# Attention products with v, retention scores and k-v products placed in larger groups, weight splits of four blocks

## Chip, core and metric

One Trainium2 chip, one core. The time is the device time of one execution in microseconds. Before the change it was 1318.73 us, the median of 3 runs (1318.46 to 1319.16). The engines have short names: PE is TensorE (matrix products), DVE is VectorE, ACT is ScalarE, POOL is GpSimd, and SP is SyncE, which issues the transfers (DMA).

## What is computed

One inference step of a two-layer encoder over 512 prompt frames and 32 sample frames, 544 columns in all, model width 1024. Each layer runs three branches side by side, merges them through gates, and ends in a layer norm. Cut to what matters here:

```python
def layer(x, pe, pos, w_in, rel_table, ...):
    u = x @ w_in
    qa, ka, va, za, qb, kb, vb, zb, xr, zc, ga, gb, gc = split_cols(u)
    # A: softmax attention with a bias by distance
    scores = einsum(qa * d ** -0.5, ka) + rel_bias;  ya = softmax(scores) @ va
    ya = ya * silu(za)
    # B: retention in blocks, rotary q and k
    inner = einsum('bnihd,bnjhd->bnhij', qb, kb) * decay
    y_in  = einsum('bnhij,bnjhe->bnihe', inner, vb)
    kv    = einsum('bnjhd,bnjhe,hj->nbhde', kb, vb, zeta)   # then a scan gives s_prev
    y_x   = einsum('bnihd,nbhde,hi->bnihe', qb, s_prev, xi)
    yb = group_norm_heads(y_in + y_x) * silu(zb)
    # C: conv and a gated linear recurrence, yc = ... * silu(zc)
    merged = sigmoid(ga) * (ya @ w_branch[0]) + sigmoid(gb) * (yb @ w_branch[1]) + sigmoid(gc) * (yc @ w_branch[2])
    r = ALPHA * x + merged @ w_out
    r = r + sigmoid(r @ w_ple_gate) * (pe @ w_ple)
    return layer_norm(r, ln_gain, ln_bias), ...
```

There are 8 heads of width 64 in A and in B. All of it is in f32; the prompt and the sample share the weights.

## The kernel before, in words

**Main stream.** All large weights are cut into blocks of 128 x 128 and stored in the order in which they are used; eight blocks are a chunk of 512 KB. A weight block and an activation are each held as a sum of two reduced-precision parts, h and lo (names ending in h and l). `block` (line 244) multiplies h by xh, h by xl and lo by xh, each over the 544 columns in two spans of 288 and 256: six products, all recorded under line 253. A unit of work (`layer_units`) is one tile of 128 output rows, with 2, 4 or 8 blocks accumulated in PSUM, after which `evac` takes the result out.

**Weights.** `load` (line 189) brings a chunk into a buffer of the pool `wr` (the name raw, four buffers; the DMA is line 201). `split` (line 206) makes two blocks at a time: a cast on ScalarE gives h (line 208), a subtraction on VectorE gives lo (line 209). Both go to the pool `wp` (wh and wl), or, for the gate weights and those of the last products of a layer, to a slab (held). `stream` (line 216) runs the splits ahead of use, at least `LEAD` = 8 blocks, and calls `load` for the next chunk when the last part of one is split. `split_ahead` (line 235) loads and splits the first four chunks of layer 1 while the end of layer 0 runs; their DMA is line 238.

**Order.** It is written out by hand: the instructions of each engine run in the order in which the program emits them. Small jobs (Python generators) run beside the main stream. `tick` is called once per block; each job says with `yield n` that it goes on n blocks later, and `PACE` holds these numbers. So what a job emits at once stands as a small group between the products of two blocks.

**Attention.** `attn_job` (line 362) adds a step every 8 blocks (`PACE["step"]`), three steps for each of four head pairs, for query tiles (0, 1), (2) and (3). `attn_step` (line 380) emits the scores of both heads (line 393, name sc), then the softmax on VectorE and ScalarE, then for each head the transposes of the probabilities (line 409, name tp) with a copy back, and at the end the products with v (line 420, name pv, probabilities sx, v as vatok). From its scores to its products with v a step lasts 14 blocks, so two steps overlap. `sample_job` does the same for the 32 sample frames (scores L450, cached keys kvc).

**Retention.** `ret_job` forms k-v products per block of frames (line 583), the running states, then for each of four head pairs the scores (line 646, QB and KB), a mask on VectorE, the products with v (line 660, inner) and with the states (line 664), both into one PSUM tile.

In the profile's rows a product has the part of the array that it uses: 128\*128 is the whole array, 128\*64 one half of its columns, 64\*128 one half of its rows.

Of the kernel before, what the change touches and what calls it, by code (L numbers as in the profile page):

```python
# [55 lines left out]
def blocks_of(kind):  # L56
# [67 lines left out]
def encoder(ctx: ExitStack, tc, xT, pT, W, RB, KC, VC, PAR, CST, LGB, o_y, o_k, o_v, o_rp, o_rs, o_cv, o_lr):  # L124
# [5 lines left out]
    slab = pool("slab", 15)  # L130
    wr = pool("wr", 4)
    wp = pool("wp", LEAD // 2 + 3)
    tp_ = pool("tmp", 13)
    sm = pool("sm", 6)
# [70 lines left out]

    def split(n, h, lo):
        t = raw[n // 8][:, n % 8:n % 8 + 2]
        S.copy(h, t)  # L208
        V.tensor_tensor(lo, t, h.bitcast(F32), SUB)  # L209
        parts[n // 2] = (h, lo)  # L210

    def hold(n):
        held[n // 8] = sl("held", F32R, (128, 2, 8, 128))
        return [[held[n // 8][:, i, k:k + 2] for i in range(2)] for k in range(0, 8, 2)]

    def stream(lead=LEAD):
        while at["split"] < L * NB and at["split"] <= at["use"] + at["more"] + lead:
            n = at["split"]
            kind, f, k = BLOCKS[n % NB]
            if n // 2 not in parts:  # L220
                if kind == "wg" or kind == "pg" and f >= HELD[n // NB]:
                    if n % 8 == 0:
                        at["hold"] = hold(n)
                    h, lo = at["hold"][n % 8 // 2]
                else:
                    h = wp.tile([128, 2, 128], F32R, tag="wh", name="wh")
                    lo = wp.tile([128, 2, 128], F32R, tag="wl", name="wl")
                split(n, h, lo)
                if n % 8 == 6:
                    load()  # L230
            at["split"] += 2


    def split_ahead(l):
        for c in range((l + 1) * NCH, (l + 1) * NCH + (AT["xr"] + 16) // 8):
            t = wr.tile([128, 8, 128], F32, tag="raw", name="raw")
            raw[c] = t
            Q.dma_start(out=t, in_=W[c // NCH, c % NCH])
            views = hold(8 * c)
            yield 8  # L240
            for i, v in enumerate(views):
                split(8 * c + 2 * i, *v)
                yield 3

    def block(ps, xh, xl, first, last, hfs=(0, 1), n=None):
        if n is None:
            n = at["use"]
            at["use"] += 1
        h, lo = parts[n // 2]
        for i, (w, x) in enumerate(((h, xh), (h, xl), (lo, xh))):  # L250
            for hf in hfs:
                a, b = SPANS[hf]
                T.matmul(ps[:, MM0 + a:MM0 + b], lhsT=w[:, n % 2, :], rhs=x[:, a:b],  # L253
                         start=first and i == 0, stop=last and i == 2)
# [38 lines left out]
    for k in range(0, 8, 2):  # L293
        if k < 6:
            load()
        Q.dma_start(out=x0[k // 4][:, k % 4:k % 4 + 2], in_=xT[:, k:k + 2])
# [23 lines left out]
    def layer(l, env, nxt):  # L320
# [40 lines left out]
        def attn_job():  # L361
            while not all(k in env for k in ("vatok", "gates", ("K", 0))):
                yield 2
            env["ya"] = sl("ya")
            bias_loads(0)
            yield 4
            for p in range(4):
                while ("K", p) not in env:
                    yield 2
                for j in range(2):  # L370
                    G.memset(env["bias", p, j][0:64, 448:512], NEG)
                for qs in ((0, 1), (2,), (3,)):
                    if qs[0] == 2 and p < 3:
                        bias_loads(p + 1)
                    add(attn_step(p, qs))
                    yield PACE["step"]
            yield PACE["attn_end"]
            env["ya1"] = True

        def attn_step(p, qs):  # L380
            QTh, QTl, KTh, KTl = (env[k] for k in ("QTh", "QTl", "KTh", "KTl"))
            scs, xs, todo = [psum("sc") for _ in range(2)], [], []
            o = 0
# [22 lines left out]
            for j in range(2):  # L406
# [3 lines left out]
                copy("p%d" % j)(xs[j][:, :o], tp[:, :o])  # L410
                yield PACE["at3"]
            if qs[0] == 0:
                env["pv"] = psum("pv")
# [72 lines left out]
        def lru_tile(t):  # L486
# [12 lines left out]
            for g in range(2):  # L499
                w, lo = ([parts[(l * NB + AT["wg"] + g * 4 + t) // 2][i][:, t % 2] for i in range(2)])  # L500
                ps = psum("sc"), psum("pv")
# [61 lines left out]
        def ret_job():  # L563
# [13 lines left out]
            kvs = tmp("kvs", (128, 4, 64))  # L577
            for c in range(5):
                ps = psum("sc")
                for p in range(4):  # L580
                    for j in range(2):
                        hs = slice((2 * p + j) * 64, (2 * p + j) * 64 + 64)
                        T.matmul(ps[64 * j:64 * j + 64, p * 64:p * 64 + 64],  # L583
                                 lhsT=kt[:, c, hs] if c < 4 else kts[:, hs],
                                 rhs=vt[:, c, hs] if c < 4 else vts[:, hs], tile_position=(0, 64 * j))
                copy("kv")(kv[:, 4 * c:4 * c + 4] if c < 4 else kvs, ps[:, :256].rearrange("p (a b) -> p a b", a=4))
                yield PACE["kv"]
            mu = sm.tile([128, 64], F32, tag="mu", name="mu", bufs=1)
# [50 lines left out]
            yield 2  # L639
            for p in range(4):  # L640
                inn, scs = [], [psum("sc") for _ in range(2)]
                for c in range(4):
                    cc = slice(c * 128, c * 128 + 128)
                    for j in range(2):
                        r = slice(64 * j, 64 * j + 64)
                        T.matmul(scs[j][:, cc], lhsT=KB[r, p, cc], rhs=QB[r, p, cc])  # L646
                for sc in scs:
                    x = tmp("inner", (128, 512))
# [5 lines left out]
                pv = psum("pv")  # L654

                for c in range(4):
                    cc = slice(c * 128, c * 128 + 128)
                    for j in range(2):
                        h = 2 * p + j
                        T.matmul(pv[64 * j:64 * j + 64, cc], lhsT=vt[:, c, h * 64:h * 64 + 64], rhs=inn[j][:, cc],  # L660
                                 start=c == 0, stop=False)
                for c in range(1, 4):
                    cc = slice(c * 128, c * 128 + 128)
                    T.matmul(pv[:, cc], lhsT=std[:, (c - 1) * 4 + p], rhs=QB[:, p, cc], start=False, stop=c == 3)  # L664
                copy("yb")(QB[:, p, :NP], pv)
# [440 lines left out]
```

## Time and profile before

| | |
|---|---|
| time, median of 3 runs | 1318.73 us |
| the profiled execution | 1319.27 us |
| its span in the trace | 1317.2 us |
| granted TensorE clock, mean | 0.997 |
| DMA queue with the weights, share of 16 engines | 28.8% |
| HBM read and written over the span | 91 GB/s |

The span runs from the first to the last event of the trace; the execution's own time is 2.1 us longer. Busy time is a share of the whole span; which engine sets the end is read from what each one waits for. In a timeline row the columns are the start, the time from the first start to the last end, the engine, the line of the kernel, the operation, what it writes and reads, the shape, and how many instructions the row holds; in brackets stands the idle time before it and what ended it. The rows overlap on TensorE, since products are pipelined, so durations there are read from start to start.

### The profile page before, as it was taken

The page shows a single profiled execution, that of the slowest core. Times are in us where ns is not written, and L with a number is a line of the kernel's source. Part 1 is how long each engine was busy: PE and PEld are TensorE (multiplying, and loading weights), DVE is VectorE, ACT ScalarE, POOL GpSimd, SP SyncE. Part 2 cuts the span into 40 slices and gives each one's busy share as a digit, 9 for nine tenths or more (in the row PEclk, how much of TensorE's full clock was granted, in tenths as well). Part 3 has the DMA queues.
Part 4 walks back from the last instruction along what each step waited for, and adds up shares of the span by engine and source line. Part 5 has one row for each costly group of instructions (what it writes and reads, how often), then busy time and mean ns, then how long its engine had stood idle before and what let it go on. Part 6 is the DMA issues. An engine that isn't in the chain of part 4 may idle for free.

```text
span 1317.2 us, 26576 instructions
## 1 busy us (share of the span) xinstructions
PE 1299.4 (99%) x10744; PEld 1265.1 (96%) x10744; DVE 757.1 (57%) x1649; ACT 581.5 (44%) x1447; POOL 164.4 (12%) x158
## 2 busy tenths in 40 slices
PE   9999999999999999999999999999999999999996
PEld 9998889999999999999989998999999999999996
DVE  5666563583764453466584765636638544444567
ACT  6765544432742233334277655444326423333341
POOL 0210030320101101100032101213201011010000
PEclk9999999999999999999999999999999999999998
DMA  7233422231122222224212345132212222222221
GB/s 296 65 131 92 162 67 94 86 105 50 65 97 97 82 80 97 94 99 145 65 47 68 115 98 177 61 99 81 89 65 75 87 96 81 97 81 97 81 97 68
DMA packets 43465, 125.96 MB, mean 96 GB/s; under 512 B 9360, under 2 KB 11664, under 8 KB 42576
## 3 DMA queue, kind: packets, MB, share of 16 engines
q1 hardware_dynamic: 43344, 124.29, 28.8%
q8 instruction: 84, 1.38, 0.4%
q14 instruction: 37, 0.30, 0.1%
HBM read 112.57 MB, written 7.24 MB: 91 GB/s over the span
## 4 chain that ended last, share of the span: by engine, by line
PE 81%; DVE 4%; ACT 2%; issue 1%; DVEq 0%; POOL 0%; ACTq 0%
PE mm L253 72%; PE pv L420 1%; PE tp L409 1%; PE sc L393 1%; PE sc L646 1%; PE tp L329 1%; PE pv L660 1%; PE pv L664 1%; PE sc L583 0%; ACT wh L208 0%; PE sc L721 0%; PE sc L476 0%; DVE tk L807 0%; DVE tk L814 0%; DVE xl L262 0%
## 5 line engine op out<-in xcount | busy, mean ns | idle before, releaser
L209 DVE TENSOR_TENSOR wl<-raw,wh 128x256 fp32r<-128x256 f32 x704 | 304.9, 468 | 298.8 <-ACT wh L208 298.2
L253 PE MATMUL mm<-xh,wh 128*128 128x288 f32 x2144 | 457.9, 295 | 0.4 <-ACT xrp L866 0.4
L253 PE MATMUL mm<-xh,wl 128*128 128x288 f32 x2144 | 444.1, 288 | 0.0
L253 PE MATMUL mm<-xl,wh 128*128 128x288 f32 x2144 | 442.7, 288 | 0.0
L253 PEld LDWEIGHTS mm<-xh,wh 128*128 128x128 f32 x2144 | 328.0, 189 | 13.8 <-issue 10.0
L253 PEld LDWEIGHTS mm<-xl,wh 128*128 128x128 f32 x2144 | 328.7, 188 | 0.0
L253 PEld LDWEIGHTS mm<-xh,wl 128*128 128x128 f32 x2144 | 328.6, 188 | 0.0
L208 ACT CAST wh<-raw 128x256 fp32r<-128x256 f32 x704 | 251.0, 403 | 53.1 <-PE mm L253 49.3
L888 ACT ACTIVATE sg<-mm 128x544 f32<-128x544 f32 x48 | 30.1, 626 | 145.2 <-PE mm L253 145.2
L900 POOL TENSOR_TENSOR m<-m,sg 128x544 f32<-128x544 f32 x30 | 42.6, 1420 | 314.0 <-DVE sg L898 314.0
L354 ACT ACTIVATE sx<-sx,sst 128x128 f32<-128x128 f32 (+4 forms) x68 | 37.9, 558 | 68.8 <-DVE sst L352 65.2
L253 PE MATMUL mm<-xh,held 128*128 128x288 f32 (+1 forms) x320 | 64.0, 291 | 0.3 <-ACT ple L908 0.3
L253 PE MATMUL mm<-mh,wh 128*128 128x288 f32 (+1 forms) x256 | 52.8, 288 | 0.0
L253 PE MATMUL mm<-mh,wl 128*128 128x288 f32 (+1 forms) x256 | 52.8, 287 | 0.0
L253 PE MATMUL mm<-ml,wh 128*128 128x288 f32 (+1 forms) x256 | 52.8, 287 | 0.0
L253 PEld LDWEIGHTS mm<-xh,held 128*128 128x128 f32 x320 | 51.3, 188 | 0.6 <-ACT ple L908 0.5
L253 PE MATMUL mm<-xl,held 128*128 128x288 f32 (+1 forms) x160 | 46.4, 290 | 0.5 <-DVE xl L262 0.4
L898 DVE TENSOR_TENSOR sg<-mm,sg 128x544 f32<-128x544 f32 x32 | 23.2, 725 | 41.2 <-PE mm L253 41.2
L261 ACT CAST xh<-r 128x544 fp32r<-128x544 f32 (+2 forms) x32 | 17.0, 531 | 67.5 <-DVE r L915 63.5
L253 PEld LDWEIGHTS mm<-ml,wh 128*128 128x128 f32 x256 | 39.2, 188 | 0.0
L253 PEld LDWEIGHTS mm<-mh,wh 128*128 128x128 f32 x256 | 39.1, 188 | 0.0
L253 PEld LDWEIGHTS mm<-mh,wl 128*128 128x128 f32 x256 | 39.0, 188 | 0.0
(251 smaller groups left out, 1760.9 us busy)
## 6 DMA issues: line engine op xcount, KB each, us to landing
raw<-in_W SPq DMA_DIRECT2D x189, 512.0 KB, 3.3
bias<-in_RB SPq DMA_DIRECT2D x16, 256.0 KB, 4.0
x<-in_xT SPq DMA_DIRECT2D x4, 544.0 KB, 9.9
o_v<-VA SPq DMA_DIRECT2D x2, 1088.0 KB, 4.6
o_k<-KT SPq DMA_DIRECT2D x2, 1088.0 KB, 5.3
swap<-KB SPq DMA_DIRECT2D x32, 68.0 KB, 2.7
swap<-QB SPq DMA_DIRECT2D x32, 68.0 KB, 2.0
o_y<-tk SPq DMA_DIRECT2D x6, 256.0 KB, 2.0
```

What stands on the lines that cost most here:

```text
L208: S.copy(h, t)
L209: V.tensor_tensor(lo, t, h.bitcast(F32), SUB)
L253: T.matmul(ps[:, MM0 + a:MM0 + b], lhsT=w[:, n % 2, :], rhs=x[:, a:b], start=first and i == 0, stop=last and i == 2)
L261: S.copy(h, src)
L329: T.transpose(tp[:rows, t * 128:(t + 1) * 128], src[:, t, c0:c0 + rows], ident)
L354: S.activation(x, x, AF.Exp, bias=s[:, 0:1], scale=-1.0, accum_out=s[:, 1:2])
L393: T.matmul(scs[j][:, o:o + n], lhsT=q_[r, p, i * 128:i * 128 + 128], rhs=k_[r, p, :n], start=k == 0, stop=k == 2)
L409: T.transpose(tp[:, c:c + 128], xs[j][:, c:c + 128], ident)
L420: T.matmul(pv[64 * j:64 * j + 64, i * 128:i * 128 + 128], lhsT=env["vatok"][:, kt, h * 64:h * 64 + 64], rhs=xs[j][:, o:o + 128], start=kt ...
L888: S.activation(sg, pv, AF.Sigmoid)
L898: V.tensor_tensor(sg, pv, sg, MUL)
L900: (V if kind == "bB" and t == 7 else G).tensor_tensor(m, m, sg, ADD)
```

## The change

It has five parts. The products with v of an attention step are no longer emitted at the step's end; they are kept in a list (`env["pvs"]`) and emitted by `flush` at the start of the step after the next, directly ahead of that step's scores. The last two are emitted together. `attn_end` goes from 17 to 9. In retention, the k-v products of two blocks of frames go into one PSUM tile, the products with the states stand ahead of the inner ones, and the scores of the next head pair follow the inner products at once; the first scores come four blocks behind the sample's masks. Splits take four blocks at a time (but two in the very first chunk), for which `wp` has 4 buffers of four blocks where it had 7 of two. There are 14 temporary buffers in place of 13, and 3 raw ones in place of 4; at the start one chunk less is loaded ahead.

```diff
-    "va0": 5, "va": 3, "step": 8, "attn_end": 17, ...
+    "va0": 5, "va": 3, "step": 8, "attn_end": 9, ...
...
-    wr = pool("wr", 4)
-    wp = pool("wp", LEAD // 2 + 3)
-    tp_ = pool("tmp", 13)
+    wr = pool("wr", 3)
+    wp = pool("wp", LEAD // 4 + 2)
+    tp_ = pool("tmp", 14)
...
-    def split(n, h, lo):
-        t = raw[n // 8][:, n % 8:n % 8 + 2]
-        S.copy(h, t)
-        V.tensor_tensor(lo, t, h.bitcast(F32), SUB)
-        parts[n // 2] = (h, lo)
+    def split(n, h, lo, step=4):
+        for k in range(0, 4, step):
+            t = raw[n // 8][:, n % 8 + k:n % 8 + k + step]
+            S.copy(h[:, k:k + step], t)
+            V.tensor_tensor(lo[:, k:k + step], t, h[:, k:k + step].bitcast(F32), SUB)
+        parts[n // 4] = (h, lo)
...
-                    h = wp.tile([128, 2, 128], F32R, tag="wh", name="wh")
-                    lo = wp.tile([128, 2, 128], F32R, tag="wl", name="wl")
-                split(n, h, lo)
-                if n % 8 == 6:
+                    h = wp.tile([128, 4, 128], F32R, tag="wh", name="wh")
+                    lo = wp.tile([128, 4, 128], F32R, tag="wl", name="wl")
+                split(n, h, lo, 2 if n < 8 else 4)
+                if n % 8 == 4:
                     load()
-            at["split"] += 2
+            at["split"] += 4
...
             for i, v in enumerate(views):
-                split(8 * c + 2 * i, *v)
-                yield 3
+                split(8 * c + 4 * i, *v)
+                yield 6
...
-        if k < 6:
+        if k < 4:
             load()
...
             yield PACE["attn_end"]
+            flush()
             env["ya1"] = True
+
+        def flush():
+            while env["pvs"]:
+                env["pvs"].pop(0)()
 
         def attn_step(p, qs):
             QTh, QTl, KTh, KTl = (env[k] for k in ("QTh", "QTl", "KTh", "KTl"))
+            flush()
             scs, xs, todo = [psum("sc") for _ in range(2)], [], []
...
+            env["pvs"].append(lambda: attn_pv(p, qs, xs))
+
+        def attn_pv(p, qs, xs):
             if qs[0] == 0:
                 env["pv"] = psum("pv")
...
-            for c in range(5):
+            for cs in ((0, 1), (2, 3), (4,)):
                 ps = psum("sc")
...
-            for p in range(4):
-                inn, scs = [], [psum("sc") for _ in range(2)]
+            def scores(p):
+                scs = [psum("sc") for _ in range(2)]
                 for c in range(4):
                     cc = slice(c * 128, c * 128 + 128)
                     for j in range(2):
                         r = slice(64 * j, 64 * j + 64)
                         T.matmul(scs[j][:, cc], lhsT=KB[r, p, cc], rhs=QB[r, p, cc])
+                return scs
+
+            yield 4
+            scs = scores(0)
+            for p in range(4):
+                inn = []
...
+                for c in range(1, 4):
+                    cc = slice(c * 128, c * 128 + 128)
+                    T.matmul(pv[:, cc], lhsT=std[:, (c - 1) * 4 + p], rhs=QB[:, p, cc], start=c == 1, stop=False)
                 for c in range(4):
                     cc = slice(c * 128, c * 128 + 128)
                     for j in range(2):
                         h = 2 * p + j
                         T.matmul(pv[64 * j:64 * j + 64, cc], lhsT=vt[:, c, h * 64:h * 64 + 64], rhs=inn[j][:, cc],
-                                 start=c == 0, stop=False)
-                for c in range(1, 4):
-                    cc = slice(c * 128, c * 128 + 128)
-                    T.matmul(pv[:, cc], lhsT=std[:, (c - 1) * 4 + p], rhs=QB[:, p, cc], start=False, stop=c == 3)
+                                 start=False, stop=c == 3)
+                if p < 3:
+                    scs = scores(p + 1)
```

**Where instructions stand, TensorE in attention.** Before, in layer 0's first head pair, the products of query tile (2) with v (six in the program) stand between two blocks of the main stream (mm, six products per block):

```order
L253 MATMUL mm<-xl,wh 128x256
L253 MATMUL mm<-xh,wl 128x288
L253 MATMUL mm<-xh,wl 128x256
L420 MATMUL pv<-sx,vatok 64x128 x6
L253 MATMUL mm<-xh,wh 128x288
L253 MATMUL mm<-xh,wh 128x256
```

After the change, the same six products stand two steps' starts on, between the transposes of the next step and the scores of the one behind that:

```order
L254 MATMUL mm<-xh,wl 128x288
L254 MATMUL mm<-xh,wl 128x256
L418 MATMUL tp<-cst,sx 128x128 x4
L432 MATMUL pv<-sx,vatok 64x128 x6
L402 MATMUL sc<-KTh,QTh 128x128 x2
L402 MATMUL sc<-KTh,QTl 128x128 x2
L402 MATMUL sc<-KTl,QTh 128x128 x2
L402 MATMUL sc<-KTh,QTh 128x256 x2
L402 MATMUL sc<-KTh,QTl 128x256 x2
L402 MATMUL sc<-KTl,QTh 128x256 x2
L254 MATMUL mm<-xh,wh 128x288
```

The transposes and scores stood next to each other before as well; the products with v have moved in between, and their own place in the stream is gone.

**TensorE in retention.** Before, the inner products and those with the states of one head pair, one block, and the scores of the next pair:

```order
L253 MATMUL mm<-xh,wl 128x256
L660 MATMUL pv<-inner,vbtok 64x128 x8
L664 MATMUL pv<-QB,states 128x128 x3
L253 MATMUL mm<-xh,wh 128x288
L253 MATMUL mm<-xh,wh 128x256
L253 MATMUL mm<-xl,wh 128x288
L253 MATMUL mm<-xl,wh 128x256
L253 MATMUL mm<-xh,wl 128x288
L253 MATMUL mm<-xh,wl 128x256
L646 MATMUL sc<-QB,KB 128x128 x8
```

After:

```order
L254 MATMUL mm<-xh,wl 128x256
L679 MATMUL pv<-QB,states 128x128 x3
L684 MATMUL pv<-inner,vbtok 64x128 x8
L661 MATMUL sc<-QB,KB 128x128 x8
L254 MATMUL mm<-xh,wh 128x288
```

The states have moved to the front, and the scores of the next pair one block forward to the inner products.

**ScalarE at the end of layer 0.** Here the casts of layer 1's first chunks (held) stand between those of the running weights (wh). The names after "waits" are semaphores; DMAHW is the landing of a load. Before:

```order
L261 CAST xh<-r 128x544 [waits DVE_49]
L208 CAST wh<-raw 128x256 [waits DMAHW0_49,PE_49,Activation_49]
L208 CAST held<-raw 128x256 [waits DMAHW3_49]
L208 CAST wh<-raw 128x256 [waits PE_49,Activation_49]
L208 CAST held<-raw 128x256
```

After:

```order
L262 CAST xh<-r 128x544 [waits DVE_49]
L209 CAST wh<-raw 128x512 [waits DMAHW0_49,PE_49,Activation_49]
L209 CAST held<-raw 128x512 [waits DMAHW2_49]
L209 CAST wh<-raw 128x512 [waits PE_49,Activation_49]
L209 CAST held<-raw 128x512
```

The order is the same with twice the width; in both, a cast of a running weight stands behind a held cast that waits for its load.

More of the change, by code (lines that the diff above doesn't have):

```diff
@@ L204, in load @@
             at["load"] = c + 1
-    def split(n, h, lo):
-        t = raw[n // 8][:, n % 8:n % 8 + 2]
-        S.copy(h, t)
-        V.tensor_tensor(lo, t, h.bitcast(F32), SUB)
-        parts[n // 2] = (h, lo)
+    def split(n, h, lo, step=4):
[4 more added lines that the diff above has]
+        parts[n // 4] = (h, lo)
     def hold(n):
         held[n // 8] = sl("held", F32R, (128, 2, 8, 128))
-        return [[held[n // 8][:, i, k:k + 2] for i in range(2)] for k in range(0, 8, 2)]
+        return [[held[n // 8][:, i, k:k + 4] for i in range(2)] for k in range(0, 8, 4)]
     def stream(lead=LEAD):
@@ L219, in stream @@
             kind, f, k = BLOCKS[n % NB]
-            if n // 2 not in parts:
+            if n // 4 not in parts:
                 if kind == "wg" or kind == "pg" and f >= HELD[n // NB]:
@@ L223, in stream @@
                         at["hold"] = hold(n)
-                    h, lo = at["hold"][n % 8 // 2]
+                    h, lo = at["hold"][n % 8 // 4]
                 else:
-                    h = wp.tile([128, 2, 128], F32R, tag="wh", name="wh")
-                    lo = wp.tile([128, 2, 128], F32R, tag="wl", name="wl")
-                split(n, h, lo)
-                if n % 8 == 6:
+                    h = wp.tile([128, 4, 128], F32R, tag="wh", name="wh")
+                    lo = wp.tile([128, 4, 128], F32R, tag="wl", name="wl")
+                split(n, h, lo, 2 if n < 8 else 4)
+                if n % 8 == 4:
                     load()
-            at["split"] += 2
+            at["split"] += 4
     def split_ahead(l):
@@ L248, in block @@
             at["use"] += 1
-        h, lo = parts[n // 2]
+        h, lo = parts[n // 4]
         for i, (w, x) in enumerate(((h, xh), (h, xl), (lo, xh))):
@@ L252, in block @@
                 a, b = SPANS[hf]
-                T.matmul(ps[:, MM0 + a:MM0 + b], lhsT=w[:, n % 2, :], rhs=x[:, a:b],
+                T.matmul(ps[:, MM0 + a:MM0 + b], lhsT=w[:, n % 4, :], rhs=x[:, a:b],
                          start=first and i == 0, stop=last and i == 2)
@@ L364, in attn_job @@
             env["ya"] = sl("ya")
+            env["pvs"] = []
             bias_loads(0)
@@ L499, in lru_tile @@
             for g in range(2):
-                w, lo = ([parts[(l * NB + AT["wg"] + g * 4 + t) // 2][i][:, t % 2] for i in range(2)])
+                w, lo = ([parts[(l * NB + AT["wg"] + g * 4 + t) // 4][i][:, t] for i in range(2)])
                 ps = psum("sc"), psum("pv")
@@ L577, in ret_job @@
             kvs = tmp("kvs", (128, 4, 64))
-            for c in range(5):
+            for cs in ((0, 1), (2, 3), (4,)):
                 ps = psum("sc")
-                for p in range(4):
[L581 to L587, printed above, removed]
+                for c in cs:
+                    for p in range(4):
+                        for j in range(2):
+                            hs = slice((2 * p + j) * 64, (2 * p + j) * 64 + 64)
+                            o = c % 2 * 256 + p * 64
+                            T.matmul(ps[64 * j:64 * j + 64, o:o + 64], lhsT=kt[:, c, hs] if c < 4 else kts[:, hs],
+                                     rhs=vt[:, c, hs] if c < 4 else vts[:, hs], tile_position=(0, 64 * j))
+                m = 4 * len(cs)
+                copy("kv")(kv[:, 4 * cs[0]:4 * cs[0] + m] if c < 4 else kvs,
+                           ps[:, :64 * m].rearrange("p (a b) -> p a b", a=m))
+                yield PACE["kv"] * len(cs)
             mu = sm.tile([128, 64], F32, tag="mu", name="mu", bufs=1)
@@ L639, in ret_job @@
             yield 2
-            for p in range(4):
-                inn, scs = [], [psum("sc") for _ in range(2)]
+            def scores(p):
+                scs = [psum("sc") for _ in range(2)]
                 for c in range(4):
@@ L646, in ret_job @@
                         T.matmul(scs[j][:, cc], lhsT=KB[r, p, cc], rhs=QB[r, p, cc])
+                return scs
+            yield 4
+            scs = scores(0)
+            for p in range(4):
+                inn = []
                 for sc in scs:
```

2 rows, old and new, of the table PACE are left out of this document.

## The prediction

> **What bounds the kernel now.** I read the page first: its span and the busy shares of the engines.
>
> ```profile
> span 1317.2 us, 26576 instructions
> PE 1299.4 (99%) x10744; PEld 1265.1 (96%) x10744; DVE 757.1 (57%) x1649; ACT 581.5 (44%) x1447; POOL 164.4 (12%) x158
> ```
>
> TensorE is busy all the way; the others have half their time free. Being busy is not yet being the bound, so the second view is the list of what TensorE waited for.
>
> ```profile
> PE tp L721 <- DVE r L931: 2.0, 2, 1.4
> PE sc L774 <- DVE lnst L766: 1.5, 1, 1.5
> PE mm L253 <- ACT ple L908: 1.1, 2, 0.8
> PE tp L409 <- DVE sx L359: 0.7, 2, 0.4
> ```
>
> These are four of its eight rows (us in total, times, longest); all eight add up to 7.7 us in 1317, and none names a split weight (wh or wl). So the time is TensorE's own stream: the many block products, and the small groups that stand between them. What such a group costs shows in the third view, the timeline of TensorE. Each row is a pair of products (288 and 256 columns); the start-to-start step of undisturbed pairs is the plain rate.
>
> ```profile
> 193.92 0.41 PE L253 MATMUL mm<-xh,wh 128*128 128x288 f32 x2
> 194.17 0.41 PE L253 MATMUL mm<-xl,wh 128*128 128x288 f32 x2
> 194.42 0.41 PE L253 MATMUL mm<-xh,wl 128*128 128x288 f32 x2
> 194.76 0.88 PE L420 MATMUL pv<-sx,vatok 128*64 128x128 f32 x12
> 195.57 0.52 PE L253 MATMUL mm<-xh,wh 128*128 128x288 f32 x2
> 195.93 0.41 PE L253 MATMUL mm<-xl,wh 128*128 128x288 f32 x2
> ```
>
> A pair takes 0.25 us (193.92 to 194.17). From the pair before the group (194.42) to the second pair behind it (195.93) are 1.51 us, of which two pairs explain 0.50: a group of 12 products costs 1.01. The field 128*64 is the part of the array that is used. Around such a group the step is 0.34 on entry and 0.36 in the first pair behind it, not 0.25. The same for 16 products:
>
> ```profile
> 185.59 0.42 PE L253 MATMUL mm<-xh,wl 128*128 128x288 f32 x2
> 185.94 1.09 PE L420 MATMUL pv<-sx,vatok 128*64 128x128 f32 x16
> 186.96 0.52 PE L253 MATMUL mm<-xh,wh 128*128 128x288 f32 x2
> 187.32 0.41 PE L253 MATMUL mm<-xl,wh 128*128 128x288 f32 x2
> ```
>
> 187.32 less 185.59 less 0.50 is 1.23. Four products more cost 0.22, 0.055 each; 12 of them are 0.66, and 0.35 is left that a group pays once, for going to the other array shape and back. This 0.35 is what joining groups can save.
>
> **The change part by part.** (The trace counts a plain f32 product twice, so x6 in the program's order is x12 here.)
>
> *Joins in attention.* In the order of the instructions, the 24 groups of probabilities times v stand like this: before, 20 alone, 2 behind the sample's scores, 2 behind a transpose; after, 20 between a transpose and the scores of the step two later, and the last four as two groups of 28. A transpose uses 128*128, the products 128*64, the scores 64*128. What is new is the direct step from 128*64 to 64*128; its price s is in no row of before. Since the scores paid for entry and return already, a joined group costs its stream plus s where it cost its stream plus 0.35, and a join saves 0.35 - s. Bounds: s is not below 0, since all products still pass; nor is it above 0.35, the price of a whole trip back to the full array and out. The nearest row is the one place where two part-array groups follow each other:
>
> ```profile
> 154.57 0.42 PE L253 MATMUL mm<-xh,wl 128*128 128x288 f32 x2
> 154.92 0.69 PE L450 MATMUL sc<-kvc,qs 64*32 64x288 f32 x8
> 155.54 1.09 PE L420 MATMUL pv<-sx,vatok 128*64 128x128 f32 x16
> 156.56 0.52 PE L253 MATMUL mm<-xh,wh 128*128 128x288 f32 x2
> 156.92 0.41 PE L253 MATMUL mm<-xl,wh 128*128 128x288 f32 x2
> ...
> 150.31 0.41 PE L253 MATMUL mm<-xh,wl 128*128 128x288 f32 x2
> 150.65 0.69 PE L450 MATMUL sc<-kvc,qs 64*32 64x288 f32 x8
> 151.27 0.52 PE L253 MATMUL mm<-xh,wh 128*128 128x288 f32 x2
> 151.62 0.42 PE L253 MATMUL mm<-xl,wh 128*128 128x288 f32 x2
> ```
>
> Joined: 156.92 - 154.57 - 0.50 = 1.85. Apart: 151.62 - 150.31 - 0.50 = 0.81 for the sample's scores, and 1.23. So 0.81 + 1.23 - 1.85 = 0.19 is saved, and s = 0.16. I take that: 20 x 0.19 = 3.8. The two groups of 28 each save a whole 0.35: 0.7. The two joins with the sample's scores are lost: -0.4. Together 4.1.
>
> [...]
>
> *kv.* Of the five kv groups per layer, the four of the prompt become two.
>
> ```profile
> 251.63 0.41 PE L253 MATMUL mm<-xh,wl 128*128 128x288 f32 x2
> 251.97 0.69 PE L583 MATMUL sc<-vbtok,kbtok 128*64 128x64 f32 x16
> 252.58 0.52 PE L253 MATMUL mm<-xh,wh 128*128 128x288 f32 x2
> 252.94 0.41 PE L253 MATMUL mm<-xl,wh 128*128 128x288 f32 x2
> ```
>
> One costs 0.81, entry and return like above. Same shape twice in a row pays them once: four times 0.35 is 1.4.
>
> *Retention.* Before, scores alone 8 times, inner products with the states behind them 8 times.
>
> ```profile
> 306.38 1.09 PE L660 MATMUL pv<-inner,vbtok 128*64 128x128 f32 x16
> 307.40 0.94 PE L664 MATMUL pv<-QB,states 128*128 128x128 f32 x6
> 308.10 0.50 PE L253 MATMUL mm<-xh,wh 128*128 128x288 f32 x2
> ```
>
> Going 128*64 to 128*128 happens once in either order, so putting the states first is worth 0. What it does is to leave the inner products last, and 6 of 8 score groups follow them directly: the same step as in attention, 6 x 0.19 = 1.1. Bounds as there.
>
> *Splits of four blocks.* Casts and subtractions of 256 columns become half as many of 512.
>
> ```profile
> L209 DVE TENSOR_TENSOR wl<-raw,wh 128x256 fp32r<-128x256 f32 x704 | 304.9, 468 | 298.8 <-ACT wh L208 298.2
> L208 ACT CAST wh<-raw 128x256 fp32r<-128x256 f32 x704 | 251.0, 403 | 53.1 <-PE mm L253 49.3
> L898 DVE TENSOR_TENSOR sg<-mm,sg 128x544 f32<-128x544 f32 x32 | 23.2, 725 | 41.2 <-PE mm L253 41.2
> L261 ACT CAST mh<-m 128x544 fp32r<-128x544 f32 x16 | 10.4, 648 | 63.0 <-POOL m L900 56.4 <-DVE m L900 6.6
> ```
>
> Between the 256- and 544-wide rows, 512 columns come to 0.62 on ScalarE and 0.70 on VectorE (estimates): some 33 and 60 us less busy, on engines that do not set the end. Worth 0 on the path. The price is that the first block of a group is ready (0.62 + 0.70) - (0.40 + 0.47) = 0.45 us later. A block is three pairs, 0.75 us; splitting runs at least 8 blocks ahead in the program, 6 us, and that covers it. At the start nothing covers it: the first evacuation stands on ScalarE behind a cast, and TensorE waits for it.
>
> ```profile
> 8.81 0.40 ACT L208 CAST wh<-raw 128x256 fp32r<-128x256 f32 x1 [0.52 <-DMA raw<-in_W]
> 9.12 0.61 ACT L908 COPY ple<-mm 128x544 f32<-128x544 f32 x1
> ```
>
> The first chunk is still cast two blocks at a time, but the cast at 8.81 is of the second chunk and becomes 0.62: +0.2 us.
>
> *Three raw buffers.* A chunk of 8 blocks lasts 6 us, so a load is issued some 6 us later than with four.
>
> ```profile
> raw<-in_W SPq DMA_DIRECT2D x189, 512.0 KB, 3.3
> 608.67 0.41 ACT L208 CAST held<-raw 128x256 fp32r<-128x256 f32 x1 [3.88 <-DMA raw<-in_W]
> ```
>
> It lands in 3.3, against two chunks (12 us) of other buffers still to be used: hidden. The exception is the end of layer 0, where chunks for the next layer are loaded in between and compete for buffers. ScalarE already waited 3.88 us there, and TensorE's list has no wait for weights, so the lead covered it. With one buffer less two held chunks wait, by the order of the loads; I cost them at 0 and keep 2 us of wait for the range.
>
> *The rest.* The 14th temporary carries the probabilities that live longer. A product with v now stands ahead of its join's scores on TensorE, and everything behind would wait for its operand; that copy is issued five blocks (3.7 us) earlier, so it is done. With nothing between scores and the next transpose, the transpose comes some 1 us earlier in relation to the softmax; the listed two waits of this kind (L409, 0.7 us) come at each layer's first step, which has no product with v ahead of it either way. Shorter attn_end lets retention begin up to 8 blocks sooner, off the path. All 0.
>
> *Sum.* 4.1 + 1.4 + 1.1 - 0.2 = 6.4. The profiled execution took 1319.27 (span 1317.2 and 2.1 around it), 0.54 above the median of the runs, 1318.73: 1312.9 for it, **1312.3** for the median.
>
> **The rivals.**
>
> *The step between shapes is free (s = 0).* 26 joins save 0.16 more each, 4.2 us: 1308.1. For it: the next weights may load while the last products pass. Against: 0.16 was paid at 154.57.
>
> *The step is as dear as going home and out (s = 0.35).* 128*64 to 64*128 changes rows and columns at once. The 26 joins give nothing, so 4.9 us are missing: 1317.2, within 0.2% of before. Against: 64*32 to 128*64 also changes both, and saved 0.19.
>
> *Weights arrive late, and it ends slower.* The place is the end of layer 0, from 600 us on. There, four chunks of the next layer share three buffers with the running ones, ScalarE's casts of running weights stand behind a held cast that waits for its load, and SyncE's queue holds the next loads behind the one that waits for a buffer. If each held chunk costs TensorE the whole 3.9 us of the row at 608.67, it is 15.6 us: 1312.3 + 15.6 = 1327.9. It decides against the change when a chunk costs over 2.3 us, since four of them must eat the 6.4 gained and 2.6 more; that is where the lead left at a held cast is under 1.6 us. For it: the wait exists already, and coarser splits take 0.45 us off the lead. Against: 3.9 us passed without a wait on TensorE, and only two of the chunks lose their slack in the order of loads. A partial form, 1 to 2 us per chunk, ends at 1316 to 1320.
>
> [...]
>
> *The change does not do what it says:* the order of instructions shows the joins, so I give it no chance.
>
> **How the numbers follow.** Forecast with s near 0.16 and at most 3 us of new waits: 0.71. Free step: 0.09. Dear step: 0.07. Late weights, partial: 0.09, half of it still faster by over 0.2%, half within. Late weights in full: 0.04, slower. About 0.2% (2.6 us) is what a measurement of this kernel can tell from no change. Faster: 0.71 + 0.09 + 0.04 = 0.84; within: 0.07 + 0.05 = 0.12; slower 0.04. The range takes in both ends of s, 1308.1 to 1317.2, and leaves out only most of the late weights and what goes beyond a free step.
>
> **What would show it.** Right, if in TensorE's timeline the pair behind a transpose, products with v and scores comes about 0.19 us sooner than the two groups took apart, a kv group of 32 costs about 1.3, and TensorE's waits stay near 8 us. A first row of wh or held in that list, above all from 600 to 690 us, shows late weights; a wait of L418 for sx shows that the transposes come too early. The forecast is wrong if s is far from 0.16, which the timeline tells at once, or if the plain rate of 0.25 us a pair changes.

## The result, and the profile after

The changed kernel takes 1309.73 us (median of 6 runs, 1309.32 to 1310.36), the kernel before 1318.73 (6 runs): 9.0 us less, ratio 0.993 with a 95% interval of 0.992 to 0.994. The forecast was 1312.3 in a range of 1308.1 to 1317.2; the gain was 6.4 by forecast and 9.0 measured. The profiled execution took 1309.81 with this page:

```profile
span 1308.0 us, 25456 instructions
PE 1291.7 (99%) x10744; PEld 1263.5 (97%) x10744; DVE 717.3 (55%) x1271; ACT 546.1 (42%) x1065; POOL 177.0 (14%) x158
```

TensorE runs the same 10744 instructions in a span 9.2 us shorter, and is busy for 7.7 us less. Its list of waits (us in total, times, longest) after the change, complete:

```profile
PE tp L744 <- DVE r L954: 2.0, 2, 1.4
PE sc L797 <- DVE lnst L789: 1.5, 1, 1.5
PE mm L269 <- DVE eps L289: 1.2, 1, 1.2
PE mm L254 <- ACT ple L931: 1.0, 2, 0.7
PE mm L254 <- DVE xl L263: 0.5, 2, 0.4
PE mm L254 <- ACT xrp L889: 0.4, 1, 0.4
```

The list adds up to 6.6 us, where it was 7.7. The layer-norm rows at the top are as before. What is gone are the rows of L409, transposes that waited for the softmax (two waits, 0.7 us together) and for a copy (one, 0.4 us). How much they really cost shows in TensorE's timeline at layer 0's first transposes, before and then after the change:

```profile
102.16 0.42 PE L253 MATMUL mm<-xh,wl 128*128 128x288 f32 x2
102.96 0.90 PE L409 MATMUL tp<-cst,sx 128*128 128x128 f32 x3 [0.38 <-DVE sx L359]
103.78 0.62 PE L393 MATMUL sc<-KTh,QTh 64*128 64x384 f32 x2
...
104.68 0.52 PE L253 MATMUL mm<-xh,wh 128*128 128x288 f32 x2
105.04 0.41 PE L253 MATMUL mm<-xl,wh 128*128 128x288 f32 x2
```

```profile
102.36 0.42 PE L254 MATMUL mm<-xh,wl 128*128 128x288 f32 x2
102.61 0.49 PE L418 MATMUL tp<-cst,sx 128*128 128x128 f32 x3
103.03 0.45 PE L402 MATMUL sc<-KTh,QTh 64*128 64x384 f32 x2
...
103.76 0.52 PE L254 MATMUL mm<-xh,wh 128*128 128x288 f32 x2
104.12 0.41 PE L254 MATMUL mm<-xl,wh 128*128 128x288 f32 x2
```

From the pair ahead to the second pair behind, less 0.50, the group cost 2.38 before and 1.26 after: 1.12 less, where the bracket says 0.38. The bracket counts only the idle time right before the first transpose. The other two stretch their row from 0.49 to 0.90 and wait inside it, and the scores behind them take longer too (0.90 from their first start to the next pair, after the change 0.73). The same happens in layer 1 (2.37 before, 1.26 after). These 2.2 us were not in the forecast.

A joined group, and a k-v group of 32, after the change:

```profile
127.38 0.41 PE L254 MATMUL mm<-xh,wl 128*128 128x288 f32 x2
127.63 0.49 PE L418 MATMUL tp<-cst,sx 128*128 128x128 f32 x3
128.05 1.09 PE L432 MATMUL pv<-sx,vatok 128*64 128x128 f32 x16
129.07 0.45 PE L402 MATMUL sc<-KTh,QTh 64*128 64x384 f32 x2
...
129.79 0.52 PE L254 MATMUL mm<-xh,wh 128*128 128x288 f32 x2
130.15 0.41 PE L254 MATMUL mm<-xl,wh 128*128 128x288 f32 x2
...
230.54 0.41 PE L254 MATMUL mm<-xh,wl 128*128 128x288 f32 x2
230.88 1.15 PE L597 MATMUL sc<-vbtok,kbtok 128*64 128x64 f32 x32
231.97 0.52 PE L254 MATMUL mm<-xh,wh 128*128 128x288 f32 x2
232.33 0.41 PE L254 MATMUL mm<-xl,wh 128*128 128x288 f32 x2
```

The joined group costs 130.15 - 127.38 - 0.50 = 2.27. The same without products with v is the first step's, 1.26, and 16 products alone cost 1.23 before: 0.22 saved here; over all 20 joined groups the mean is 0.20. The k-v group costs 232.33 - 230.54 - 0.50 = 1.29 against 2 x 0.81: 0.33 saved.

### The profile page after: what moved, and what is told of

Same layout as the page of the kernel before. It is cut to its first block, busy times and chain, and to the rows that moved or that the text cites. A ratio compares the mean times of both kernels' runs of the same rounds, so it can differ in the third digit from the quotient of the medians.

```text
span 1308.0 us, 25456 instructions
## 1 busy us (share of the span) xinstructions
PE 1291.7 (99%) x10744; PEld 1263.5 (97%) x10744; DVE 717.3 (55%) x1271; ACT 546.1 (42%) x1065; POOL 177.0 (14%) x158
## 4 chain that ended last, share of the span: by engine, by line
PE 95%; DVE 3%; DMA 1%; ACT 1%; issue 0%; SPq 0%; POOL 0%; DVEq 0%
PE mm L254 84%; PE pv L432 2%; PE sc L402 2%; PE tp L418 1%; PE tp L330 1%; DMA raw<-in_W 1%; PE sc L661 1%; PE pv L684 1%; PE pv L516 0%; DVE r L813 0%; PE sc L516 0%; DVE xl L263 0%; PE sc L744 0%; PE sc L597 0%; PE pv L679 0%
## 5 line engine op out<-in xcount | busy, mean ns | idle before, releaser
L210 DVE TENSOR_TENSOR wl<-raw,wh 128x512 fp32r<-128x512 f32 (+1 forms) x354 | 261.4, 756 | 283.8 <-ACT wh L209 279.9
L209 ACT CAST wh<-raw 128x512 fp32r<-128x512 f32 (+1 forms) x354 | 208.3, 614 | 36.9 <-PE mm L254 30.8
L923 POOL TENSOR_TENSOR m<-m,sg 128x544 f32<-128x544 f32 x30 | 46.8, 1560 | 316.6 <-DVE sg L921 316.6
L565 POOL TENSOR_TENSOR swap<-swap,cst 128x544 f32<-128x544 f32 x16 | 25.3, 1580 | 109.8 <-DMA swap<-QB 68.1
L902 ACT ACTIVATE z<-mm 128x544 f32<-128x544 f32 x24 | 15.0, 626 | 59.2 <-PE mm L254 59.1
```

The lines of the kernel that those rows point to most:

```text
L209: S.copy(h[:, k:k + step], t)
L210: V.tensor_tensor(lo[:, k:k + step], t, h[:, k:k + step].bitcast(F32), SUB)
L565: G.tensor_tensor(sw, sw, cst[:, C_SIN:C_SIN + N], MUL)
L902: S.activation(z, pv, AF.Sigmoid)
L923: (V if kind == "bB" and t == 7 else G).tensor_tensor(m, m, sg, ADD)
```

## The experiments

The times beside each run are medians, and ratios are to the kernel before, timed on the same chip along with the run (1318.93 for the first four and the next four, 1318.98 for the last three). The changed kernel was not timed again beside them: its 1309.73 belongs to 1318.73, so differences to the changed kernel are uncertain by some 0.2 us. Where a group's time is given in ns, it runs from the start of the pair ahead to the start of the pair behind, less the 250 ns of one pair.

**Attention part alone.** The kernel before with `env["pvs"]`, `flush`, `attn_end` 9 and 14 temporaries; splits, raw buffers, k-v and retention as before.

```diff
-    ... "attn_end": 17, ...
+    ... "attn_end": 9, ...
...
-    tp_ = pool("tmp", 13)
+    tp_ = pool("tmp", 14)
...
+            flush()
             scs, xs, todo = [psum("sc") for _ in range(2)], [], []
...
+            env["pvs"].append(lambda: attn_pv(p, qs, xs))
```

> The kernel before with the attention part alone (products with v kept and emitted ahead of later scores, attn_end 9, 14 temporary buffers). Shape theory: 20 joins at 0.19, two groups of 28 at 0.35, two joins with the sample's scores lost: 4.1 us faster, about 1314.6, and the waits of the first transposes in each layer (L409, 0.38 and 0.36 in the list of before) stay. Rival: those waits also go because of this part, another 2.2 us: about 1312.4.

Measured: 1324.4, ratio 1.0041 (1.0028 to 1.0053), 5.5 us slower. Both theories miss. The joined groups that nothing disturbs are as cheap as in the changed kernel (2.2 to 2.3 us in both), so some 4.3 us were gained; about 9.8 were lost elsewhere. The two first rows of TensorE's list of waits name the places:

```profile
PE sc L657 <- DVE ins L648: 3.9, 2, 2.0
PE tp L417 <- ACT PT L477: 2.3, 2, 1.4
```

L657 are the first retention scores: they need a PSUM buffer that VectorE frees when it has masked the sample's scores (ins). `attn_end` 9 starts retention 8 blocks earlier, into a stretch in which VectorE still builds the states (until 282.7 us in layer 0); a multiply and three splits stand there too before the masks. L417 are transposes that need the one PSUM buffer of their kind, which ScalarE frees when it has copied the sample's probabilities (PT). In the trace the first place loses 3.6 and 4.1 us in the two layers, with the slow stretch behind each wait (granted clock 0.50 from 286 to 288 us in layer 0) that the last part describes, and the second 2.1 us more than before.

**Splits alone.** The kernel before with splits of four blocks, four raw buffers.

```diff
-    wp = pool("wp", LEAD // 2 + 3)
+    wp = pool("wp", LEAD // 4 + 2)
...
-                    h = wp.tile([128, 2, 128], F32R, tag="wh", name="wh")
+                    h = wp.tile([128, 4, 128], F32R, tag="wh", name="wh")
```

> The kernel before with splits of four blocks alone (four raw buffers, 16 blocks of split weights). Recorded prediction: nothing but the later start, 1318.9. Theory from the profile after: with half as many subtractions, none that waits for a cast stands ahead of the first softmax of a layer on VectorE, and the two first transposes no longer stall (2265 and 2252 ns for the group before, 1146 and 1146 after): 2.2 us faster less up to 0.4 at the start, about 1316.5 to 1317.0.

Measured: 1316.83, ratio 0.9983 (0.9974 to 0.9992), 2.1 us faster. No transpose of the attention waits any more: L409 is not in its list, nor is its new line. The recorded "worth 0" is wrong.

**k-v alone.** The kernel before with the k-v products of two blocks of frames in one group.

```diff
-            for c in range(5):
+            for cs in ((0, 1), (2, 3), (4,)):
```

> The kernel before with the joined k-v groups alone. Shape theory: four entries and returns at 0.35 less, 1.4 us faster, about 1317.3; a group of 32 costs 1.27 to 1.28 with its return where two of 16 cost 0.81 each. Rival, that a group costs only its products: 1318.7.

Measured: 1317.45, ratio 0.9988 (0.9980 to 0.9997), 1.5 us faster, as the shape theory has it.

**Retention alone.** The kernel before with the states first, the scores of the next pair behind the inner products, and the first scores later.

```diff
+            yield 4
+            scs = scores(0)
...
+                if p < 3:
+                    scs = scores(p + 1)
```

> The kernel before with the retention part alone (states first, scores of the next pair behind the inner products, first scores four blocks later). Recorded prediction: 6 joins at 0.19, 1.1 us faster, 1317.6; from the profile after 6 x 0.22 and 0.3 at each layer's last groups, 1.6 us, 1317.1. Rival, that states first costs an extra change of shape: 1318.7 or more.

Measured: 1317.36, ratio 0.9988 (0.9979 to 0.9997), 1.6 us faster. States first cost nothing: a group of states and inner products with no scores behind it takes 1.90 us in the changed kernel, 1.89 before in the other order.

**Products with v ahead of the transposes.** The changed kernel; `flush` moves from the start of a step to the transposes of the step before, in the same tick.

```diff
-            flush()
             scs, xs, todo = [psum("sc") for _ in range(2)], [], []
...
             for j in range(2):
+                if j == 0:
+                    flush()
                 tp = psum("tp")
```

> The changed kernel with one thing moved: at the same tick the products with v stand ahead of the transposes instead of behind them, so 128*64, 128*128, 64*128 in place of 128*128, 128*64, 64*128. The same instructions in the same number of groups. If a join saves because it drops a change of array shape: 20 changes come back, 20 x 0.197 = 3.9 us slower than the changed kernel, 1313.6. If it saves because the main stream is broken into fewer times: no difference, 1309.7.

Measured: 1313.09, 3.4 us slower than the changed kernel. Products stand between the blocks in as many groups as there, and no row of this run's list of waits is one of the attention, so it is the order of shapes that counts. One group in the timeline of this run:

```profile
110.07 0.41 PE L254 MATMUL mm<-xh,wl 128*128 128x288 f32 x2
110.41 0.88 PE L433 MATMUL pv<-sx,vatok 128*64 128x128 f32 x12
111.22 0.55 PE L419 MATMUL tp<-cst,sx 128*128 128x128 f32 x3
111.70 0.50 PE L401 MATMUL sc<-KTh,QTh 64*128 64x512 f32 x2
...
112.59 0.53 PE L254 MATMUL mm<-xh,wh 128*128 128x288 f32 x2
```

2.52 us from the pair ahead to the pair behind. The same group of the changed kernel took 2.37: 109.97 to 112.34. One change of shape more costs 0.15, times 20 is 3.0. The rest is the last two steps of each layer, whose products with v are now two groups instead of one of 28.

**Narrow splits.** The changed kernel with splits of two blocks again; all else kept, three raw buffers too.

```diff
-                split(n, h, lo, 2 if n < 8 else 4)
+                split(n, h, lo)
```

> The changed kernel with splits of two blocks again (three raw buffers, all joins and paces kept). If the wide splits took away waits: the first transposes stall again (2 x 1.1 us) and the sample's transposes as in the run of the attention part alone (1.1 and 1.6): 1312 to 1314.6. If the splits are worth nothing (recorded): 1309.5 to 1309.7.

Measured: 1314.54, 4.8 us slower than the changed kernel. Both kinds of transposes wait again: the first ones of each layer (2273 and 2252 ns for a group of 1146), and those behind the sample's (3.34 and 3.39 us, from the pair ahead to the second pair behind less 0.50, for 2.23). Together these four are 4.5 of the 4.8 us. TensorE and ScalarE at the latter place in this run:

```profile
163.54 0.49 PE L474 MATMUL tp<-cst,sx 128*128 128x128 f32 x3
166.43 0.55 PE L417 MATMUL tp<-cst,sx 128*128 128x128 f32 x3 [0.90 <-ACT PT L477]
```

```profile
164.95 0.62 ACT L354 ACTIVATE sx<-sx,sst 128x384 f32<-128x384 f32 x1 [3.00 <-DVE sst L352]
...
165.57 0.39 ACT L208 CAST wh<-raw 128x256 fp32r<-128x256 f32 x1
165.86 0.36 ACT L476 COPY PT<-tp 128x256 f32<-128x256 f32 x1
166.13 0.25 ACT L477 COPY PT<-tp 32x128 f32<-32x128 f32 x1
```

The sample's transposes were done at 164.0, but their copy stands on ScalarE behind an exponential that waits 3.00 us for VectorE, and behind a cast. After the change the same two copies run at 163.57 and 163.83, before the next transposes are due. With three raw buffers and narrow splits no row of this run's list names a weight: three raw buffers in place of four bring no wait here.

**Scores at once.** The changed kernel without the four blocks ahead of the first retention scores.

```diff
-            yield 4
             scs = scores(0)
```

> The changed kernel without the four blocks between the sample's masks and the first retention scores. If these four blocks hide the wait seen in the run of the attention part alone (3850 and 3957 ns where such a group takes 1183): 3 to 5.5 us slower than the changed kernel, 1312.7 to 1315.2. If VectorE, with half as many subtractions, is early enough without them: 1309.7.

Measured: 1315.74, 6.0 us slower than the changed kernel, a little beyond the first theory. The wait is back (L661 for ins, 3.3 us in two times), and more follows it. TensorE's timeline, layer 0:

```profile
280.63 0.41 PE L254 MATMUL mm<-xh,wl 128*128 128x288 f32 x2
282.68 1.35 PE L661 MATMUL sc<-QB,KB 64*128 64x128 f32 x16 [1.64 <-DVE ins L652]
283.96 0.77 PE L254 MATMUL mm<-xh,wh 128*128 128x288 f32 x2
284.53 0.66 PE L254 MATMUL mm<-xl,wh 128*128 128x288 f32 x2
284.99 0.66 PE L254 MATMUL mm<-xh,wl 128*128 128x288 f32 x2
```

The pairs behind the wait start 0.46 us apart instead of 0.25, at a granted clock of 0.50 (285 to 287 us). The last part of this text comes back to this.

**More joins.** The changed kernel with all k-v groups of a layer in one, and the sample's two score groups in one.

```diff
+            pss = []
             for cs in ((0, 1), (2, 3), (4,)):
-                ps = psum("sc")
+                ps = psum("tp" if cs[0] == 4 else "sc")
...
+                pss.append(ps)
+            for cs, ps in zip(((0, 1), (2, 3), (4,)), pss):
...
+                scs.append(sc)
+            for j, sc in enumerate(scs):
                 xs.append(exps(tmp("sx", (128, PAST + NS)), sc[:, :PAST + NS], sb[j]))
```

> The changed kernel with two more joins: all five k-v groups of a layer in one, and the sample's two score groups in one. Shape theory per layer: 0.35 for the two groups of 32, 0.2 for the fifth group with its other shape, 0.35 for the sample's scores, 1.8 us for two layers: 1307.9. Rival: the sample's softmax or the copies come later and a wait takes it back: 1309 to 1311.

Measured: 1309.7, no gain. The k-v groups of a layer went from 2 x 1174 + 703 to 2716 ns, as expected. But the sample's second scores wait for a PSUM buffer that the softmax of the running step still holds (L462 for sst, 1.2 us in two times): their joined group takes 1987 ns where two took 711 each.

**Attention part and four blocks.** The first run, with the first retention scores four blocks later.

```diff
-            yield 2
+            yield 6
             for p in range(4):
                 inn, scs = [], [psum("sc") for _ in range(2)]
```

> The kernel before with the attention part, and the first retention scores four blocks behind the sample's masks. If those masks cost the attention part alone 2.7 us per layer and some aftermath: 5.5 to 6 us faster than it (1324.4), 1318.4 to 1318.9, with the waits of the transposes for the sample's copy (1.1 and 1.6 us) still there. Rival: the slowness has another cause, and it stays above 1321.

Measured: 1317.93, ratio 0.9994 (0.9985 to 1.0003), 6.5 us faster than the attention part alone, half a microsecond beyond the theory, so that cause holds. Against the kernel before, 1.0 us faster is not clear of noise: the interval takes in 1, and the 11 executions lie between 1316.3 and 1320.5. The transposes behind the sample's wait even longer here (groups of 4234 and 3226 ns for 2120).

**k-v and the sample's products.** The changed kernel with the k-v groups in one, and the sample's retention products behind the last inner ones; the sample's scores left as they were.

```diff
                 if p < 3:
                     scs = scores(p + 1)
+                else:
+                    pt = psum("tp")
...
-            S.copy(QB[:, :, NP:], pv[:, :128].rearrange("p (a b) -> p a b", a=4))
+            S.copy(QB[:, :, NP:], pt[:, :128].rearrange("p (a b) -> p a b", a=4))
```

> The changed kernel with the five k-v groups of a layer in one, and the sample's retention products (in the transposes' PSUM slot) behind the last inner products; the sample's scores as in the changed kernel. Shape theory: 2 x 0.55 (measured in the run with more joins: 2716 ns for 2 x 1174 + 703, and two returns) and 2 x 0.2: 1.5 us faster than the changed kernel, about 1308.2. Rival: a new wait takes it back, 1309.7 or more.

Measured: 1308.26 (1307.94 to 1308.63), ratio to the kernel before 0.9919 (0.9905 to 0.9933): 1.5 us faster than the changed kernel, and the fastest of all.

**Two halves.** The changed kernel, each split of four blocks as two casts and two subtractions of 256 columns, emitted together.

```diff
-                split(n, h, lo, 2 if n < 8 else 4)
+                split(n, h, lo, 2)
...
-                split(8 * c + 4 * i, *v)
+                split(8 * c + 4 * i, *v, 2)
```

> The changed kernel, where each split of four blocks is made as two casts and two subtractions of 256 columns, emitted together: the places in the program are those of the changed kernel, the instructions as wide as before. If the place counts (no subtraction between the softmax's maximum and its division that waits for a cast): 1309.7 to 1310.5. If the width counts (time of VectorE and ScalarE): towards the run with narrow splits, 1313 to 1314.5.

Measured: 1315.04, 5.3 us slower than the changed kernel, and slower than either theory had it. So the place alone does not do it; but the list of waits shows that each counts somewhere:

```profile
PE tp L418 <- ACT PT L478: 1.3, 2, 0.9
...
PE mm L254 <- ACT wh L209: 0.8, 2, 0.4
```

The first transposes of a layer no longer wait (1225 and 1146 ns): there the place decides. Those behind the sample's wait as with narrow splits (3224 and 2799 ns for 2120), and now the main stream waits for a weight near 273 and 923 us (0.95 us lost at each): there it counts that the splits are twice as many instructions. On VectorE two halves took 0.76 us at 273.96, little more than the 0.68 of one whole, but far longer at two other places. Ahead of the sample's copy, and GpSimd at that time:

```profile
160.04 1.85 DVE L210 TENSOR_TENSOR wl<-raw,wh 128x256 fp32r<-128x256 f32 x2
160.26 1.35 POOL L570 TENSOR_TENSOR KB<-KB,cst 128x512 f32<-128x512 f32 x1 [7.30 <-DVE KB L567]
```

Here the two halves take 1.85 us; the one whole of the changed kernel takes 0.68 at the same place (from 160.34), with the same GpSimd work running from 160.56 to 162.17. Ahead of the weight near 273, four halves beside GpSimd's subtractions take 3.96 us (from 266.00), two wholes 2.98 (from 264.45 after the change, GpSimd's subtractions until 266.87). Whether GpSimd's work stretches them was not shown: no run moved it away. And 1.1 of the 5.2 us by which this profile's span is longer come after TensorE's last product, where no split is left.

## Why the prediction was right, and where it was not

**Joins in attention (4.1).** Right. In the two traces: 20 x 0.20, 2 x 0.35 for the groups of 28, less 2 x 0.20 for the lost joins, 4.3 us. The price s, of the step from 128\*64 to 64\*128, came out as 0.35 - 0.20 = 0.15, against 0.16 taken. The order of shapes, not the number of groups, makes it: the run with products with v ahead of the transposes brings 0.15 back per group.

**k-v (1.4).** Right: four times 0.33, 1.3, and 1.5 by the run of this part alone.

**Retention (1.1).** Slightly low: 6 x 0.20, and 0.25 that was not in the sum, at each layer's last group, the sample's products (1712 ns before, 1588 after); why these are cheaper stays open. Alone it measured 1.6. States first was indeed worth nothing.

**Splits (0 on the path).** This is the step that failed: "some 33 and 60 us less busy, on engines that do not set the end. Worth 0 on the path." The busy time fell by about as much (35 us on ScalarE, 40 on VectorE, all changes together), but these engines did set TensorE's pace: at the first transposes of both layers, and in layer 0 at those behind the sample's. With it failed the step on the waits of L409, of which the forecast said "L409, 0.7 us" and that they come "either way": they went, and they had cost 2.2 us. The first transposes wait because VectorE, before, stood idle for 1.62 us until 100.45, at a subtraction whose cast was late:

```profile
98.41 0.42 DVE L352 CUSTOM_DVE_ANT_0 sx<-sc,bias 128x256 f32<-128x256 f32 x1
...
100.45 0.42 DVE L209 TENSOR_TENSOR wl<-raw,wh 128x256 fp32r<-128x256 f32 x1 [1.62 <-ACT wh L208]
100.79 1.22 DVE L537 TENSOR_TENSOR_SCAN lru_i<-lru_a,lru_r 128x512 f32<-128x512 f32 x1
```

That cast stood on ScalarE behind a table load of 1.28 us and the two exponentials of the softmax, from 97.84 to 100.03. With splits of four blocks no subtraction stands at this place: the scan starts at 98.26, and the division of the softmax comes early enough. Another 0.6 us came from a transpose that waited for the sample's copy before (a group of 1897 ns for 1312). The splits of four blocks also lost something: 0.4 us at the layer norm's transposes near 623 us (a group of 720 ns for 353).

**Start (-0.2).** The size fits. The product behind the wait for the first evacuation starts at 10.05 us where it started at 9.78, and 0.20 of that is left at the first attention scores (95.59 and 95.39). But the longest wait for an evacuation (ple) lay between 0.3 and 1.5 us in the profiles of the study, so this is not settled.

**Sum.** 4.3 + 1.3 + 1.5 + 2.2 + 0.6 - 0.4 - 0.2 is 9.3; the last block product starts 9.2 us earlier in the trace. The joins, which the forecast was made of, came out close to their size; the rest of the gain is waits that it had put at nothing. That the time still lies in the range is luck in part: its lower end was worked out from a free step, and no bound stood for waits that go away.

**The rest (all 0).** Right in its sum, for a reason not given. An earlier retention is not off the path: in the run of the attention part alone its first scores wait, 2.7 us in each layer by the group's time. The four blocks ahead of the first scores, which the forecast passed over, hide it. The parts are not additive either: attention with four blocks (1.0, within its noise), splits (2.1), k-v (1.5) and retention (1.6) sum to 6.2 of 9.0. The difference is about the wait for the sample's copy, which attention lengthens and splits of four blocks take away: 2.1 + 1.1 us in the run of attention with four blocks.

**The rivals.** The free step forecast 1308.1, near the time measured, but s is 0.15; that the time is near is chance. The dear step fell with the same number. Late weights did not happen, though ScalarE's waits for loads came as foreseen. ScalarE at the end of layer 0 after the change:

```profile
605.36 0.62 ACT L209 CAST held<-raw 128x512 fp32r<-128x512 f32 x1 [4.33 <-DMA raw<-in_W]
620.26 0.62 ACT L209 CAST held<-raw 128x512 fp32r<-128x512 f32 x1 [4.96 <-DMA raw<-in_W]
```

Two long ones, and no wait for a weight on TensorE. VectorE and ScalarE were at 57% and 44% and did make TensorE wait; wider instructions took the waits of the transposes away, and breaking those up in place (two halves) cost 5.3 us.

## What to carry to other kernels

Groups of products in another array shape are best placed side by side, and in an order that changes the shape as seldom as possible: in this kernel a join of attention saved 0.20 us, and one change of shape more cost 0.15. The saving of a join can be read from the trace before it is made (0.19 here). A bracket in a timeline row counts only the idle time ahead of its first instruction (0.38 us where the group lost 1.12): compare the whole group with an undisturbed one of its kind. When a job is moved earlier, look at what the engine that feeds it does at that time, and do not call an engine free because its share of busy time is half (57% for VectorE here, where splits of four blocks alone gained 2.1 us). What counts is what stands in its queue at the places where the bound engine needs it.

## What the runs showed of the hardware

After some waits TensorE ran slower for a while. Two waits of near length show it: 1.64 us, until 282.68, in the run with scores at once, and 1.90 us, until 167.43, in the run of attention with four blocks (stretches of 1 us; columns: stretch, its length, busy time and count of PE, PEld, DVE, ACT and POOL, granted clock, DMA share, GB/s):

```profile
281.00:282.00 1.00, 0.04 (x1) 0.00 (x0) 1.00 (x3) 0.00 (x0) 0.00 (x0) 1.00 0.00 0
282.00:283.00 1.00, 0.32 (x3) 0.32 (x5) 0.82 (x3) 0.00 (x0) 0.00 (x0) 1.00 0.37 45
283.00:284.00 1.00, 1.00 (x17) 0.88 (x15) 0.13 (x1) 0.00 (x0) 0.00 (x0) 1.00 0.77 270
284.00:285.00 1.00, 1.00 (x6) 1.00 (x6) 0.56 (x1) 0.00 (x0) 0.00 (x0) 0.52 0.57 225
285.00:286.00 1.00, 1.00 (x6) 1.00 (x6) 0.00 (x0) 0.00 (x0) 0.00 (x0) 0.50 0.00 0
286.00:287.00 1.00, 1.00 (x6) 1.00 (x6) 0.00 (x0) 0.00 (x0) 0.00 (x0) 0.50 0.00 0
287.00:288.00 1.00, 1.00 (x8) 1.00 (x8) 0.00 (x0) 0.91 (x2) 0.00 (x0) 0.77 0.00 0
```

```profile
166.00:167.00 1.00, 0.00 (x0) 0.00 (x0) 0.01 (x1) 1.00 (x4) 0.79 (x1) 1.00 0.00 0
167.00:168.00 1.00, 0.57 (x5) 0.40 (x7) 1.00 (x3) 1.00 (x4) 0.00 (x0) 1.00 0.00 0
168.00:169.00 1.00, 1.00 (x14) 0.83 (x16) 0.88 (x4) 0.56 (x2) 0.00 (x0) 1.00 0.40 102
169.00:170.00 1.00, 1.00 (x9) 0.59 (x8) 0.30 (x1) 0.00 (x0) 0.00 (x0) 1.00 0.97 332
170.00:171.00 1.00, 1.00 (x11) 0.99 (x10) 0.40 (x2) 0.51 (x1) 0.00 (x0) 1.00 0.87 288
```

Behind the wait of 1.64 us the granted clock fell to 0.50 and was back at 1.00 from 288 us on; about seven pairs cost 0.2 us more each, 1.4 us, nearly the price of the wait itself. The clock fell in layer 1 of this run too (mean 0.83 from 930 to 940 us), and in both layers of the attention part alone (waits of 3.9 us in two times, longest 2.0; means 0.68 from 284 to 288 and 0.60 from 940 to 944). Yet the wait of 1.90 us was followed by pairs at the full rate, 0.25 us apart, with a granted clock of 1.00.

What decides between the two was not shown: no run set out to move a wait or to change its length. One program also differs from execution to execution: the five of the attention part alone took from 1322.5 us at a mean clock of 0.997 to 1326.8 at 0.992.
